# Full-width rectangles in a gated recurrence, and a different order of loads and splits at the ends of a two-layer decoder kernel

## The chip, the core and the metric

The kernel runs on one core of a Trainium2 chip. The core has a matrix engine (TensorE, PE in the profile, with its weight loads shown apart as PEld), a vector engine (DVE), a scalar engine (ACT), a general engine (POOL), and a queue that only issues transfers here (SP). They run side by side and wait for each other through semaphores; each of them takes its own instructions in a fixed order. The metric is the device time of one launch in microseconds.

## The reference

Input x is 1024 tokens of 1024 features; 16 learned meta tokens are put in front. Two layers follow, each `h = h + mixer(rmsnorm(h) * w)`, then a last rmsnorm of the 1024 real tokens. Everything is float32.

Layer 0 (pooling mixer): `v, gate = split(h @ w_in)` with 2048 columns each. In four groups of 512 channels, u is the trailing mean of v over 2, 4, 8 or 16 tokens less v itself. Each group goes through its own 512 x 512 matrix, is scaled, multiplied by `silu(gate)` and goes through `w_out` (2048 to 1024).

Layer 1 (HGRN2): `q, f, i, gate = split(h @ w_in)` with 2048 columns each, in 16 heads of 128. Per head and token the state is `S_t = diag(f_t) S_(t-1) + k_t i_t^T` and the output `o_t = S_t^T q_t`, with `f = lb + (1 - lb) sigmoid(fp)` and `k = (1 - lb) sigmoid(-fp)`. The output is normed per head, multiplied by `silu(gate)` and goes through `w_out`.

## The kernel before

**Precision and products.** The large products run on operands split into a high and a low part (`split`, L147: ACT casts the high part, DVE subtracts it to get the low one), three matmuls for one. The two input products use Strassen's scheme: a pair of weight blocks (`pair`, L213) gives seven operands P1 to P7, made one after the other from two raw tiles of 512 KB, and `products` (L364) runs them in the order P1, P2, P6, P5, P7, P3, P4 against the token operands `T`. The tokens are handled in two halves of 520 (`passes`), each in two chunks of 260 columns; a product is 12 matmuls for one half, 24 for both.

**Weights.** `feed` is a list of functions, each of which makes one split weight operand. `fill` keeps up to three (`LOOK`) made ahead; `need` hands out the next. A split operand lies in one of five "w" buffers (`wslot`), a raw weight tile in one of three "raw" buffers. The first pair of layer 0 stands twice in the list: once for the first half of the tokens, once for the second, since the second half's `T` is not ready when the first half's products start. For layer 1 that holds for the first two pairs.

**Tokens.** `tokens` (L308) gives a list of steps for one half, five tiles of up to 128 tokens. `first(i)` loads the x rows into "ht", in layer 1 adds the transposed output of layer 0 (`ys`, L324, L328) and stores the sum to DRAM (L330), squares it with a running sum on ACT (L331), makes the reciprocal root (DVE L105, POOL L106) and scales the rows (ACT L333). `second(i)`, two steps later, transposes the tile on PE in two halves of a PSUM bank each (L346) and multiplies by the norm weights, half of it on ACT (L349), half on DVE (L351). `make_T` follows: sums and differences of the normed blocks (L277) and their splits.

**The recurrence.** For each head `scan` (L742) lists pieces that are put in between the next head's products; PIECES gives the tick at which each of them is issued, and a tick follows every product (in the last stage every weight tile). Scores inside a chunk of 128 tokens are built in a matrix A: 32 x 32 diagonal blocks by masked 128 x 128 products (L683), then `rect` (L625) at width h = 32 and h = 64, which computes for each chunk the block of h keys by the h queries after them. At h = 32 it does so in two groups of 8 chunk matmuls (keys 0 to 31 and 64 to 95), each with its ACT copy (L636), at h = 64 in one. All groups write the same PSUM bank. These matmuls are plain float32, two instructions each. `states` (L776) makes the chunk sums K^T V: the first from the 16 meta rows (L785), the rest from 128 rows (L787). `outs` multiplies A and V, Q and S (L808, L809), `gated` turns the normed output, multiplies by the gate and stores it to DRAM (L832).

**The last stage.** `out1` (L886) takes the token tiles in three rounds of 3, 3 and 2. For each of 16 heads it reads the gated output back from DRAM (L904), splits it, and multiplies it by `hgrn_w_out`, which is split in the first round and kept. The last head's pieces are issued there, one tick for each weight tile; what has not been issued when the last head's operand is due is issued at once (`flush`, L895).

**Order.** The program's order is a priority. The framework lays out each engine's and each queue's instruction list when the kernel is built, by priority and by when its planner expects operands and buffers; at run time nothing is reordered. Buffers of one tag ("u": 38 of one token-length row each) are handed out in the order in which the program asks for them.

The functions that the change touches:

Of the kernel before, what the change touches and what calls it, by code (L numbers as in the profile page):

```python
# [51 lines left out]
def kernel(  # L52
# [102 lines left out]
    def whole(fast):  # L155
# [24 lines left out]
        def ensure(i):  # L180
            for j in range(len(raws), min(i + 1, len(raw_views))):
                raws[j] = rawtile()
                v = raw_views[j]
                nc.sync.dma_start(raws[j].rearrange("p (a b) -> p a b", b=v.shape[2]), v)

        def fill():
            while feed and len(fed) < LOOK:
                fed.append(feed.pop(0)())

        def need():  # L190
            if not fed:
                fed.append(feed.pop(0)())
            return fed.pop(0)
# [7 lines left out]
        def wslot():  # L201
            return wp.tile([P, 2, 512], F32R, tag="w", name="w", bufs=5)
# [105 lines left out]
        def tokens(p, w, ys=None):  # L308

            hn, held = [], {}  # L310

            def first(i):
                t0, tn = TP[p][i]
                o = t0 - p * PT
                ht, sq = unit("ht"), unit("sq")
                src = meta_tokens if t0 == 0 else x[t0 - META : t0 - META + tn]
                nc.sync.dma_start(ht[:tn, :D], src)
                ssq, r = small("ssq", 3), small("rstd", 3)
# [12 lines left out]
                act.activation(sq[:tn, :D], ht[:tn, :D], AF.Square, accum_out=ssq[:tn, 0:1])  # L331
                rstd_into(r, ssq, tn, 1, D)
                act.activation(sq[:tn, :D], ht[:tn, :D], AF.Copy, scale=r[:tn, 0:1])  # L333
                held[i] = sq

            def second(i):
                if not hn:
                    hn.extend(unit("hn").rearrange("p (k t) -> p k t", k=2) for _ in range(4))
                t0, tn = TP[p][i]
                o = t0 - p * PT  # L340
                xt = held.pop(i)
                for h in range(2):
                    b = atbank().rearrange("p (k t) -> p k t", t=P)
                    for k in range(4):
                        kk = h * 4 + k
                        pe.transpose(out=b[:, k, :tn], in_=xt[:tn, kk * P : (kk + 1) * P], identity=ident[:tn, :tn])  # L346
                    for k in (0, 1):
                        kk = h * 4 + k
                        act.activation(hn[2 * h][:, k, o : o + tn], b[:, k, :tn], AF.Copy, scale=w[:, kk : kk + 1])  # L349
                    ww = w[:, h * 4 + 2 : h * 4 + 4].unsqueeze(2).to_broadcast([P, 2, tn])  # L350
                    vec.tensor_tensor(hn[2 * h + 1][:, :, o : o + tn], b[:, 2:4, :tn], ww, mul)  # L351

            n = len(TP[p])
            steps = []
            for i in range(n + 2):
                def step(i=i):
                    if i < n:
                        first(i)
                    if i >= 2:
                        second(i - 2)  # L360
                steps.append(step)
            return steps + make_T(p, hn)

        def products(passes, m, m2):  # L364
# [3 lines left out]
            for name in PRODUCTS:  # L368
                w = need()
# [180 lines left out]
        def view1(t):  # L550
            return [cols(w_in1, "qfig".index(part) * ME + t // 2) for part in ("qg", "fi")[t % 2]]

        def mixer1(steps):
# [71 lines left out]
            def rect(Q, K0, h):  # L625

                b = atbank()
                for s0 in range(0, P, 2 * h):
                    for c in range(NT):
                        pe.matmul(  # L630
                            b[s0 : s0 + h, c * h : (c + 1) * h],
                            lhsT=K0[:, c * P + s0 : c * P + s0 + h],
                            rhs=Q[:, c * P + s0 + h : c * P + s0 + 2 * h],
                            start=True, stop=True,
                        )
                    act.copy(  # L636
                        A.rearrange("p (c t) -> p c t", t=P)[s0 : s0 + h, :, s0 + h : s0 + 2 * h],
                        b[s0 : s0 + h, : NT * h].rearrange("p (c i) -> p c i", i=h),
                    )
# [102 lines left out]
            def scan(n, Q, K, F, ti):  # L742
# [6 lines left out]
                def turn_v():  # L749
                    V = tl["V"] = unit("V")[:, :SEQ].rearrange("p (c v) -> p c v", v=P)  # L750
                    Vm = tl["Vm"] = cst.tile([P, P], F32, tag="Vm", name="Vm", bufs=2)
                    for b0 in (0, 4, 8):
# [42 lines left out]
                def outs():  # L795
# [5 lines left out]
                    ssq, r = small("ssq", 3), small("rstd", 3)  # L801
# [21 lines left out]
                def gated():  # L823
# [8 lines left out]
                    nc.sync.dma_start(a_dram[n], og)  # L832
# [53 lines left out]
        def out1():  # L886
# [6 lines left out]
            def prep(r, n):  # L893
# [9 lines left out]
                ar = half("ar").rearrange("p a b -> p (a b)")[:, : nt * P]  # L903
                nc.sync.dma_start(ar, a_dram[n][:, t0 * P : (t0 + nt) * P])  # L904
# [21 lines left out]
            for r, (tt0, nt) in enumerate(ROUNDS):  # L926
                ps = {}
                for n in range(HEADS - 3):
# [7 lines left out]
                    tick()  # L936
                fetch((r + 1) * HEADS + 2)
                late = [ready.pop((r, n)) for n in range(HEADS - 3, HEADS)]
                for i in range(nt):
# [5 lines left out]
                    ssq, rs = small("ssq", 3), small("rstd", 3)  # L945
# [27 lines left out]
        early(1, ME, lambda t: (cols(w_in0, t), cols(w_in0, ME + t)))  # L973
# [10 lines left out]
        spread(tokens(1, nw[0]))  # L984
        c0 = v_gate(0)
        products((0,), *c0)
        flush()
        products((1,), *c0)
# [5 lines left out]
        a = grp_stage(0)  # L994
        hs = out_stage(0, a)
# [4 lines left out]
        mixer1(tokens(1, nw[1], hs))  # L1000
# [38 lines left out]
```

## Time and profile before

| what | value |
|---|---|
| median of 3 runs | 1800.05 us (1799.66 to 1802.28) |
| the profiled execution | 1796.19 us, span 1794.4 us |
| PE busy | 1701.6 us, 95% of the span |
| DVE, ACT, POOL busy | 1238.1, 807.7, 51.8 us |
| granted TensorE clock, mean | 0.981 |

The span is what the profiler sees of one execution; the device time has 1.8 us more around it. In views by instruction a row gives start, length, engine, line, operation, operands, count, and in brackets how long the engine had been idle and what ended that. In the chain of waits a row gives start, length and what the end of the program waited for at that time. The granted clock is 1.00 at full speed and 0.50 at half.

### The profile page before, as it was taken

The page shows a single profiled execution, that of the slowest core. Times are in us where ns is not written, and L with a number is a line of the kernel's source. Part 1 is how long each engine was busy: PE and PEld are TensorE (multiplying, and loading weights), DVE is VectorE, ACT ScalarE, POOL GpSimd, SP SyncE. Part 2 cuts the span into 40 slices and gives each one's busy share as a digit, 9 for nine tenths or more (in the row PEclk, how much of TensorE's full clock was granted, in tenths as well). Part 3 has the DMA queues.
Part 4 walks back from the last instruction along what each step waited for, and adds up shares of the span by engine and source line. Part 5 has one row for each costly group of instructions (what it writes and reads, how often), then busy time and mean ns, then how long its engine had stood idle before and what let it go on. Part 6 is the DMA issues. An engine that isn't in the chain of part 4 may idle for free.

```text
span 1794.4 us, 32938 instructions
## 1 busy us (share of the span) xinstructions
PE 1701.6 (95%) x13571; PEld 1634.3 (91%) x13571; DVE 1238.1 (69%) x1948; ACT 807.7 (45%) x1783; POOL 51.8 (3%) x70
## 2 busy tenths in 40 slices
PE   3699999999999999699999999999999999999897
PEld 2599999999999899599999999999999999987686
DVE  4676777789226824798887887887887887783332
ACT  5643333335225624545544555544554544553221
POOL 0110000000000000000000000000000000000000
PEclk9699999999999999899999999999999999999999
DMA  3232333349337434122212212222212212351531
GB/s 91 71 113 96 107 107 110 104 148 302 107 119 232 123 95 125 63 86 78 66 61 83 84 48 78 66 70 73 83 50 81 72 60 72 108 191 50 166 106 40
DMA packets 194083, 178.68 MB, mean 100 GB/s; under 512 B 7189, under 2 KB 167013, under 8 KB 193925
## 3 DMA queue, kind: packets, MB, share of 16 engines
q1 hardware_dynamic: 193925, 176.49, 31.0%
q8 instruction: 109, 1.79, 0.4%
q14 instruction: 49, 0.40, 0.1%
HBM read 134.13 MB, written 42.34 MB: 98 GB/s over the span
## 4 chain that ended last, share of the span: by engine, by line
PE 86%; DVE 6%; DMA 3%; ACT 3%; issue 1%; POOL 1%; SPq 0%; DVEq 0%; POOLq 0%; ACTq 0%
PE mm L383 17%; PE mm L385 17%; PE mm L384 17%; PE mm L505 5%; PE mm L506 5%; PE mm L507 5%; PE mm L922 3%; PE mm L924 3%; PE mm L923 3%; PE at L630 2%; DMA ht<-in_x_dram 2%; PE at L683 2%; PE at L787 2%; PE at L809 2%; PE at L808 2%
## 5 line engine op out<-in xcount | busy, mean ns | idle before, releaser
L383 PE MATMUL mm<-Th,w 128*128 128x260 f32 x2688 | 781.1, 291 | 24.9 <-ACT Th L148 9.4
L385 PE MATMUL mm<-Th,w 128*128 128x260 f32 x2688 | 768.9, 286 | 0.6 <-DVE w L149 0.5
L384 PE MATMUL mm<-Tl,w 128*128 128x260 f32 x2688 | 765.2, 285 | 1.9 <-DVE Tl L149 1.9
L383 PEld LDWEIGHTS mm<-Th,w 128*128 128x128 f32 x2688 | 512.6, 191 | 31.6 <-ACT Th L148 10.8
L384 PEld LDWEIGHTS mm<-Tl,w 128*128 128x128 f32 x2688 | 513.2, 191 | 3.0 <-DVE Tl L149 2.9
L385 PEld LDWEIGHTS mm<-Th,w 128*128 128x128 f32 x2688 | 512.4, 191 | 2.3 <-DVE w L149 1.4
L149 DVE TENSOR_TENSOR w<-raw,w 128x512 fp32r<-128x512 f32 x351 | 235.2, 686 | 182.7 <-ACT w L148 180.5
L148 ACT CAST w<-raw 128x512 fp32r<-128x512 f32 x351 | 212.8, 620 | 166.2 <-PE mm L507 106.4
L505 PE MATMUL mm<-a,w 128*128 128x260 f32 x512 | 145.0, 283 | 0.0
L506 PE MATMUL mm<-a,w 128*128 128x260 f32 x512 | 144.6, 282 | 0.0
L507 PE MATMUL mm<-a,w 128*128 128x260 f32 x512 | 144.2, 282 | 0.0
L389 ACT COPY P<-mm 128x520 f32<-128x520 f32 (+1 forms) x153 | 85.9, 562 | 120.1 <-PE mm L385 118.6
L148 ACT CAST w<-S 128x512 fp32r<-128x512 f32 x102 | 61.3, 620 | 119.4 <-PE mm L385 61.2
L664 DVE RECIPROCAL F<-X 128x260 f32<-128x260 f32 x64 | 111.3, 1758 | 0.0
L922 PE MATMUL mm<-woh,w 128*128 128x512 f32 x256 | 103.7, 405 | 5.3 <-ACT w L148 3.6
L924 PE MATMUL mm<-woh,w 128*128 128x512 f32 x256 | 102.2, 400 | 0.0
L923 PE MATMUL mm<-wol,w 128*128 128x512 f32 x256 | 102.0, 398 | 0.0
L506 PEld LDWEIGHTS mm<-a,w 128*128 128x128 f32 x512 | 96.5, 188 | 0.0
L507 PEld LDWEIGHTS mm<-a,w 128*128 128x128 f32 x512 | 96.4, 188 | 0.0
L505 PEld LDWEIGHTS mm<-a,w 128*128 128x128 f32 x512 | 96.4, 188 | 0.0
L106 POOL TENSOR_TENSOR rstd<-rstd,nhalf 128x1 f32<-128x1 f32 (+4 forms) x44 | 44.2, 1005 | 1723.5 <-DVE rstd L105 1712.1
L505 PE MATMUL mm<-u,w 128*128 128x260 f32 x256 | 73.9, 289 | 0.5 <-ACT u L148 0.5
(147 smaller groups left out, 2509.1 us busy)
## 6 DMA issues: line engine op xcount, KB each, us to landing
raw<-in_hgrn_w_in_dram SPq DMA_DIRECT2D x68, 512.0 KB, 4.3
raw<-in_pool_w_in_dram SPq DMA_DIRECT2D x34, 512.0 KB, 4.3
raw<-in_pool_w_out_dram SPq DMA_DIRECT2D x32, 512.0 KB, 4.1
u_dram<-d SPq DMA_DIRECT2D x16, 520.0 KB, 2.7
ur<-u_dram SPq DMA_DIRECT2D x32, 260.0 KB, 5.0
sgh<-s_dram SPq DMA_DIRECT2D x32, 260.0 KB, 4.8
raw<-in_pool_w_grp_dram SPq DMA_DIRECT2D x16, 512.0 KB, 3.7
gl<-g_dram SPq DMA_DIRECT2D x32, 256.0 KB, 5.6
```

Source lines behind the costliest of these rows:

```text
L148: act.copy(hi, src)
L149: vec.tensor_tensor(lo, src, hi.bitcast(F32), sub)
L383: pe.matmul(o, lhsT=w[:, 0, ks], rhs=th[:, k], start=first, stop=False, **kw)
L384: pe.matmul(o, lhsT=w[:, 0, ks], rhs=tl[:, k], start=False, stop=False, **kw)
L385: pe.matmul(o, lhsT=w[:, 1, ks], rhs=th[:, k], start=False, stop=k == 3, **kw)
L505: pe.matmul(o, lhsT=w[:, 0, ks], rhs=xs[k][:, 0, cs], start=first and k == 0, stop=False)
L506: pe.matmul(o, lhsT=w[:, 0, ks], rhs=xs[k][:, 1, cs], start=False, stop=False)
L507: pe.matmul(o, lhsT=w[:, 1, ks], rhs=xs[k][:, 0, cs], start=False, stop=last and k == 3)
L664: vec.reciprocal(iX[:, s], X[:, s])
L922: pe.matmul(ps[i][nh], lhsT=w[:, 0, ts], rhs=wh[:, s], start=n == 0, stop=False)
L923: pe.matmul(ps[i][nh], lhsT=w[:, 0, ts], rhs=wl[:, s], start=False, stop=False)
L924: pe.matmul(ps[i][nh], lhsT=w[:, 1, ts], rhs=wh[:, s], start=False, stop=n == HEADS - 1)
```

## The change

1. `rect` multiplies, for each of the 8 chunks, all 128 key rows by 64 queries: at h = 32 the two odd blocks of 32, at h = 64 the upper 64. The result has 128 rows, of which the needed blocks are copied as before.
2. The 16-row state product gets 128 rows: POOL sets the two operands to zero before ACT writes the 16 rows.
3. In the start, the x rows of the first half are loaded first. The first two raw weight tiles wait for the reciprocal root of the second token tile, through a small DVE copy into them; behind them come the x rows of the second half.
4. The first pair of layer 0 stands once in the list. Its seven operands are kept from the first half's products for the second half's. Two of them lie in "u" buffers, and a count (`limit`) holds back further splits until kept buffers come free.
5. In layer 0 the scaling of the token rows goes from ACT to DVE. In both layers a token tile is transposed into one PSUM buffer of two banks; in layer 0 one of four pairs is multiplied on ACT and three on DVE, in layer 1 two and two.
6. In layer 1, the first three x tiles of the second half are loaded in the out stage of layer 0, and `second(i)` comes three steps after `first(i)`.
7. In the last stage there are two ticks for each weight tile. The last head's gated output stays in SBUF: it is neither stored nor read back.

The diff, cut to its core:

```diff
         def ensure(i):
             for j in range(len(raws), min(i + 1, len(raw_views))):
                 raws[j] = rawtile()
+                if j < 2:
+                    vec.tensor_copy(raws[j][:8, 0:1], stat[0][:8, 0:1])
...
+        limit, spare = [7], [2]
         def fill():
-            while feed and len(fed) < LOOK:
+            while feed and len(fed) < LOOK and limit[0] > 0:
                 fed.append(feed.pop(0)())
+                limit[0] -= 1
...
         def wslot():
+            if spare[0] > 0:
+                spare[0] -= 1
+                return unit("w", F32R)[:, :1024].rearrange("p (h k) -> p h k", h=2)
...
+        def load_tokens(p, i):
+            t0, tn = TP[p][i]
+            ht = unit("ht")
+            nc.sync.dma_start(ht[:tn, :D], meta_tokens if t0 == 0 else x[t0 - META : t0 - META + tn])
+            return ht
...
-                act.activation(sq[:tn, :D], ht[:tn, :D], AF.Copy, scale=r[:tn, 0:1])
+                if i == 1:
+                    stat[0] = r
+                if ys is None:
+                    vec.tensor_scalar(sq[:tn, :D], ht[:tn, :D], r[:tn, 0:1], None, mul)
+                else:
+                    act.activation(sq[:tn, :D], ht[:tn, :D], AF.Copy, scale=r[:tn, 0:1])
...
+                b = mmbanks().rearrange("p h (k t) -> p (h k) t", t=P)
+                for k in range(KD):
+                    pe.transpose(out=b[:, k, :tn], in_=xt[:tn, k * P : (k + 1) * P], identity=ident[:tn, :tn])
+                for j in range(4):
+                    ks = slice(2 * j, 2 * j + 2)
+                    if j == 0 or (j == 2 and ys is not None):
+                        for k in (2 * j, 2 * j + 1):
+                            act.activation(hn[j][:, k % 2, o : o + tn], b[:, k, :tn], AF.Copy, scale=w[:, k : k + 1])
+                    else:
+                        ww = w[:, ks].unsqueeze(2).to_broadcast([P, 2, tn])
+                        vec.tensor_tensor(hn[j][:, :, o : o + tn], b[:, ks, :tn], ww, mul)
...
-            for name in PRODUCTS:
-                w = need()
+            for i, name in enumerate(PRODUCTS):
+                if kept is not None and len(kept) == 7:
+                    w = kept[i]
+                    if i >= 2:
+                        limit[0] += 1
+                else:
+                    w = need()
+                    if kept is not None:
+                        kept.append(w)
...
+                if m == 5 and p == 1:
+                    ahead.extend(load_tokens(1, i) for i in range(3))
...
             def rect(Q, K0, h):
-                b = atbank()
-                for s0 in range(0, P, 2 * h):
-                    for c in range(NT):
-                        pe.matmul(
-                            b[s0 : s0 + h, c * h : (c + 1) * h],
-                            lhsT=K0[:, c * P + s0 : c * P + s0 + h],
-                            rhs=Q[:, c * P + s0 + h : c * P + s0 + 2 * h],
-                            start=True, stop=True,
-                        )
-                    act.copy(...)
+                b = atbank().rearrange("p (c i) -> p c i", i=64)
+                q4 = Q.rearrange("p (c b i) -> p c b i", c=NT, i=h)
+                for c in range(NT):
+                    pe.matmul(b[:, c], lhsT=K0[:, c * P : (c + 1) * P], rhs=q4[:, c, 1::2], start=True, stop=True)
+                A3 = A.rearrange("p (c t) -> p c t", t=P)
+                for i, s0 in enumerate(range(0, P, 2 * h)):
+                    act.copy(A3[s0 : s0 + h, :, s0 + h : s0 + 2 * h], b[s0 : s0 + h, :, i * h : (i + 1) * h])
...
+                            pool.memset(Vm, 0.0)
...
+                            pool.memset(KT[:, 7], 0.0)
...
-                                pe.matmul(b[:, c], lhsT=KT[:META, 7], rhs=Vm[:META], start=True, stop=True)
+                                pe.matmul(b[:, c], lhsT=KT[:, 7], rhs=Vm, start=True, stop=True)
...
-                    nc.sync.dma_start(a_dram[n], og)
+                    if n < HEADS - 1:
+                        nc.sync.dma_start(a_dram[n], og)
+                    else:
+                        last.append(og)
...
                         proj(ps, w, n, i)
-                    tick()
+                        if i < 2:
+                            tick()
...
-        early(1, ME, lambda t: (cols(w_in0, t), cols(w_in0, ME + t)))
+        early(0, ME, lambda t: (cols(w_in0, t), cols(w_in0, ME + t)))
...
-        for fn in tokens(0, nw[0]):
+        hts = [[load_tokens(0, i) for i in range(len(TP[0]))]]
+        for i, fn in enumerate(tokens(0, nw[0], hts=hts[0])):
             fn()
-        fill()
+            if i == 1:
+                ensure(1)
+                hts.append([load_tokens(1, i) for i in range(len(TP[1]))])
+            if i == len(TP[0]):
+                fill()
...
-        mixer1(tokens(1, nw[1], hs))
+        mixer1(tokens(1, nw[1], hs, ahead, 3))
```

## Rows read from the trace of the kernel before

**Rows 1.** The page: busy times, and the costliest groups (busy, mean ns).

```profile
PE 1701.6 (95%) x13571; PEld 1634.3 (91%) x13571; DVE 1238.1 (69%) x1948; ACT 807.7 (45%) x1783; POOL 51.8 (3%) x70
L149 DVE TENSOR_TENSOR w<-raw,w 128x512 fp32r<-128x512 f32 x351 | 235.2, 686 | 182.7 <-ACT w L148 180.5
```

**Rows 2.** Windows: stretch, length, busy PE, PEld, DVE, ACT, POOL, clock, DMA, GB/s.

```profile
14.00:38.00 24.00, 10.65 (x49) 8.88 (x50) 9.85 (x24) 17.50 (x39) 2.58 (x4) 1.00 0.27 84
38.00:99.00 61.00, 39.13 (x203) 34.13 (x203) 41.96 (x73) 38.04 (x73) 9.85 (x9) 0.72 0.24 74
710.00:740.00 30.00, 20.44 (x125) 17.18 (x124) 16.89 (x35) 18.28 (x43) 2.10 (x3) 0.77 0.40 139
740.00:770.00 30.00, 20.86 (x139) 18.68 (x138) 28.61 (x48) 16.34 (x33) 0.00 (x0) 0.93 0.16 44
```

**Rows 3.** Chain of waits in one head: start, length, what.

```profile
1080.98 1.07 PE at L630 x16
...
1129.80 0.12 PE mm L385
1129.92 0.62 PE at L630 x16
1130.54 0.33 PE mm L383
...
1134.44 1.07 PE at L630 x16
...
1142.31 0.41 PE at L785 x2
1142.73 1.76 PE at L787 x14
...
1150.26 0.22 PE at L808 x2
```

**Rows 4.** Groups by form, weight loads: count, busy us, mean ns, idle before.

```profile
L808 PEld LDWEIGHTS at<-V,A 128*128 128x128 f32 x256 | 39.0, 192 | 0.2
L630 PEld LDWEIGHTS at<-Q,K 128*32 128x32 f32 x512 | 18.6, 113 | 4.9 <-issue 0.4 <-ACT A L636 0.4
L757 PEld LDWEIGHTS at<-ident,ti 128*128 128x128 f32 x128 | 14.7, 142 | 0.1
L757 PEld LDWEIGHTS at<-ident,ti 128*16 128x16 f32 x16 | 1.4, 87 | 2.7 <-ACT V L759 2.7
```

**Rows 5.** Timeline, weight loads of a 16-token tile's transposes in layer 1.

```profile
569.54 0.32 PEld L346 LDWEIGHTS at<-ident,sq 16*128 16x128 f32 x4 [0.32 <-DVE ht L328]
```

**Rows 6.** Timeline of the start, ACT and DVE.

```profile
11.63 1.14 ACT L148 CAST w<-raw 128x512 fp32r<-128x512 f32 x2 [1.58 <-DMA raw<-in_pool_w_in_dram]
...
14.89 1.06 ACT L331 ACTIVATE sq<-ht 128x1024 f32<-128x1024 f32 x1 [1.08 <-DMA ht<-in_x_dram]
...
37.36 0.40 DVE L351 TENSOR_TENSOR hn<-at,vecs 128x240 f32<-128x240 f32 x1
```

**Rows 7.** Lines by source, whole span: count, ns min/median/max, first and last start, forms.

```profile
L333 ACT ACTIVATE sq<-ht,rstd x20: 1144/1150/1158, 12.7 to 732.4; 128x1024 f32<-128x1024 f32 x14, 16x1024 f32<-16x1024 f32 x2, 120x1024 f32<-120x1024 f32 x2, 8x1024 f32<-8x1024 f32 x2
L349 ACT ACTIVATE hn<-at,vecs x80: 246/360/407, 19.9 to 739.2; 128x128 f32<-128x128 f32 x56, 128x16 f32<-128x16 f32 x8, 128x120 f32<-128x120 f32 x8, 128x8 f32<-128x8 f32 x8
L588 DVE TENSOR_SCALAR F<-F,oml,lb x34: 408/550/555, 741.0 to 1574.0; 128x520 f32<-128x520 f32 x30, 128x260 f32<-128x260 f32 x4
```

**Rows 8.** Timeline, entry of layer 1, SP and DVE.

```profile
722.31 0.42 SPq L317 DMA_DIRECT2D ht<-in_x_dram  x1
...
728.17 1.28 DVE L328 TENSOR_TENSOR ht<-ht,at 128x512 f32<-128x512 f32 x2 [1.96 <-DMA ht<-in_x_dram]
```

**Rows 9.** Timeline, end of the first round of the last stage, PE.

```profile
1656.38 0.62 PE L829 MATMUL at<-ident,on 128*128 128x128 f32 x2 [1.80 <-ACT on L821]
...
1665.30 0.50 PE L922 MATMUL mm<-woh,w 128*128 128x512 f32 x1 [3.65 <-ACT w L148]
```

**Rows 10.** Windows, the same end.

```profile
1666.00:1670.00 4.00, 4.00 (x12) 3.23 (x12) 2.19 (x5) 1.54 (x3) 0.00 (x0) 0.59 0.96 305
```

More of the change, by code (lines that the diff above doesn't have):

```diff
@@ L192, in need @@
                 fed.append(feed.pop(0)())
+                limit[0] -= 1
             return fed.pop(0)
@@ L306, in make_T, with tokens @@
             return [s1, s2, s3, s4, s5, s6]
-        def tokens(p, w, ys=None):
+        stat = [None]
+        def load_tokens(p, i):
[3 more added lines that the diff above has]
+            return ht
+        def tokens(p, w, ys=None, hts=None, lag=2):
             hn, held = [], {}
@@ L314, in first @@
                 o = t0 - p * PT
[L315 to L318, printed above, removed]
+                ht, sq = hts.pop(0) if hts else load_tokens(p, i), unit("sq")
+                ssq, r = small("ssq", 3), small("rstd", 4)
                 if ys is not None:
@@ L341, in second @@
                 xt = held.pop(i)
[L342 to L351, printed above, removed]
+                b = mmbanks().rearrange("p h (k t) -> p (h k) t", t=P)
[9 more added lines that the diff above has]
+                        vec.tensor_tensor(hn[j][:, :, o : o + tn], b[:, ks, :tn], ww, mul)
             n = len(TP[p])
             steps = []
-            for i in range(n + 2):
+            for i in range(n + lag):
                 def step(i=i):
@@ L358, in step, with products @@
                         first(i)
-                    if i >= 2:
-                        second(i - 2)
+                    if i >= lag:
+                        second(i - lag)
                 steps.append(step)
             return steps + make_T(p, hn)
-        def products(passes, m, m2):
+        def products(passes, m, m2, kept=None):
             s = slice(passes[0], passes[-1] + 1)
             a = x_ = None
-            for name in PRODUCTS:
-                w = need()
+            for i, name in enumerate(PRODUCTS):
[7 more added lines that the diff above has]
+                        kept.append(w)
                 if name == "P1":
@@ L551, in view1 @@
             return [cols(w_in1, "qfig".index(part) * ME + t // 2) for part in ("qg", "fi")[t % 2]]
+        last = []
         def mixer1(steps):
@@ L800, in outs @@
                     on = tl["on"] = [half("on").rearrange("p a b -> p (a b)")[:, :512].rearrange("p (c v) -> p c v", v=P) for _ in range(2)]
-                    ssq, r = small("ssq", 3), small("rstd", 3)
+                    ssq, r = small("ssq", 3), small("rstd", 4)
                     tl["r"] = r
@@ L902, in prep @@
                 t0, nt = ROUNDS[r]
-                ar = half("ar").rearrange("p a b -> p (a b)")[:, : nt * P]
-                nc.sync.dma_start(ar, a_dram[n][:, t0 * P : (t0 + nt) * P])
+                ts = slice(t0 * P, (t0 + nt) * P)
+                if n < HEADS - 1:
+                    ar = half("ar").rearrange("p a b -> p (a b)")[:, : nt * P]
+                    nc.sync.dma_start(ar, a_dram[n][:, ts])
+                else:
+                    ar = last[0][:, ts]
                 w = wslot()
@@ L944, in out1 @@
                         proj(ps, w, HEADS - 3 + j, i)
-                    ssq, rs = small("ssq", 3), small("rstd", 3)
+                    ssq, rs = small("ssq", 3), small("rstd", 4)
                     for nh in range(2):
@@ L977, in whole @@
         early(2, 2 * HEADS, view1)
-        for fn in tokens(0, nw[0]):
-            fn()
-        fill()
+        hts = [[load_tokens(0, i) for i in range(len(TP[0]))]]
+        for i, fn in enumerate(tokens(0, nw[0], hts=hts[0])):
+            fn()
+            if i == 1:
[3 more added lines that the diff above has]
+                fill()
         if fast:
             later(40, make_mask)
-        spread(tokens(1, nw[0]))
-        c0 = v_gate(0)
-        products((0,), *c0)
+        spread(tokens(1, nw[0], hts=hts[1]))
+        c0, kept = v_gate(0), []
+        products((0,), *c0, kept)
         flush()
-        products((1,), *c0)
+        products((1,), *c0, kept)
+        limit[0] = len(feed)
         for t in range(1, ME):
@@ L994, in whole @@
         a = grp_stage(0)
+        ahead = []
         hs = out_stage(0, a)
```

4 lines of the change are left out of this document (removed).

## The prediction, made before the change was run

> **What bounds the kernel now.** I read the page's busy line first, then windows over the stretches in which TensorE is idle, then the chain of waits inside one recurrence head, then the timeline at the start, at the entry of the second layer and at the end. TensorE is busy for 1701.6 of 1794.4 us [rows 1], so 92.8 us are idle, and the rest can shrink only by giving TensorE less to do. The idle time is not spread: 13.4 us lie in 14 to 38, 21.9 in 38 to 99, 18.7 in 710 to 770 [rows 2]; the last head's return costs 1.80 and 3.65 more [rows 9]. Inside a head there is none: the groups and products follow each other on TensorE without a gap, and a head is 1134.44 - 1080.98 = 53.46 us [rows 3]. So three edits aim at idle time, and one (rectangles and the 16-row state product) at TensorE's own work.
>
> **The steady heads.** A product step costs 0.12 us; a group costs its own row plus what the product behind it takes above 0.12 [rows 3]. The 32-wide level runs as two groups of 16 instructions (each matmul is two), each 0.62 + (0.33 - 0.12) = 0.83, so 1.66. The 64-wide level is 1.07 + 0.2 = 1.27. Together 2.93 us a head. New: each level is 8 matmuls, 16 instructions, with 128 stationary columns and 64 moving ones. No row has that form. From below: the 64-wide group's own pace, 1.07 / 16 = 0.067 each, if the moving side sets it. From above: load and stream one after the other. What does a load cost? By form it takes 113 ns for 32 columns and 192 for 128 [rows 4], 0.82 ns a column, so 105 ns for 128 columns beyond a fixed part. That this slope is a pace and not a latency is shown by the transposes: their loads go from 87 to 142 ns between 16 and 128 columns, 0.49 ns a column, 63 ns for 128, and where the moving side is only 16 columns four of them take 0.32 us, (0.32 - 0.14) / 3 = 0.06 each [rows 5]. So a narrow moving side leaves the load as the bound. The existing full-size form, 128 columns against 128, takes 0.22 for two instructions (one of sixteen such rows of the output step [rows 3]); I take its 0.111 each for the new form too. A level is then 16 x 0.111 = 1.78, both 3.55, without the 0.2 us that stands behind the narrow groups (none stands behind the full-size ones). That is 3.55 - 2.93 = +0.62 us a head: this edit loses. Bounds: 32 x 0.067 = 2.14, -0.79 a head; one after the other 32 x (0.105 + 0.067) = 5.5, +2.6 a head.
>
> The Trainium skill, "TensorE: Matmul & The Clock Gate", section "LDWEIGHTS (loading the stationary operand)", says that a load's time goes with its columns, P / 1.2 ns, and speaks against this edit: estimated from it, 32 x 0.107 = 3.4 us a head, +0.5, about what the rows give. [...]
>
> The state product: the 16-row pair and the 14 full ones take 0.41 + 1.76 = 2.17 [rows 3]; 16 full ones at 0.111 are 1.78. That saves 0.39 a head (nothing if the extra is not due to the 16 rows, 0.41 at most). Its two memsets run on POOL, which is busy for 51.8 us in all [rows 1]; they stand before small ACT copies, but their tile is free long before, so I cost them at nothing; were POOL late, ACT's queue would wait a few tenths per head, and ACT is busy for only 45% [rows 1]. Heads: 16 x (0.62 - 0.39) = **+4 us** (from -19 to +36).
>
> **The start.** Today the first x tile is squared at 14.89, 3.3 us after the first weights were cast at 11.63 [rows 6], since two weight loads are queued ahead of it. With x first it takes the weights' place: about 11.6. The weights are then issued when the second tile's rstd is there, near 14, and come while the other tiles are worked on; their splits are not needed before the first operand is split. From 14.89 to the last normed tile at 37.36 [rows 6] the four big tiles take 22.5 us, mostly ACT, which is busy 17.5 of the 24 us from 14 to 38: square 1.06, scale 1.15, four copies of 0.36 a tile [rows 2, 6, 7]. The scale goes to DVE: TENSOR_SCALAR takes 0.41 at 260 and 0.55 at 520 columns [rows 7], so 0.55 + 504 x 0.00053 = 0.82 at 1024 (1.15, ACT's, as upper bound). One pair of ACT copies per tile becomes one DVE product of 0.40 [rows 6]. A tile is then 1.06 + 2 x 0.36 = 1.8 on ACT and 0.82 + 3 x 0.40 = 2.0 on DVE. Four tiles: 11.6, plus 6 for the first one's way through (today 22.5 less three quarters of it, 5.6), plus 3 x 2.0, is 24; with DVE also splitting weights I take 27. Gain to there 10.4 (bounds 5 and 13).
>
> From 38 to 99 (both single passes of the first pair, between them the second half's tokens) DVE is busy 41.96 of 61 us, ACT 38.04 [rows 2]. Gone: 7 splits of 0.69 [rows 1] and 4 sums of that length on DVE, 7.5 us, their ACT casts and two loads. Added on DVE: 5 x 0.82 scales and 5 products of 0.40, 6; and some 3.5 of splits that now fall behind the last tile. So DVE has 44 us, ACT only 38 - 4 - 6 - 3 = 25. DVE becomes the bound of this stretch. At the 95% it reaches in 740 to 770 [rows 2] it needs 46 us, at today's 69% 64; I take 80%, since the x rows of the second half are now there early and no cast waits for a weight slot in between: 55. Against 61 that gains 6 (bounds 15 and -3). The start: **-16 us** (-2 to -28). What is late next is DVE: the differences and splits of T.
>
> **Entry of the second layer.** Each x tile is issued behind the store of the tile before; the last one at 722.31 lands for DVE at 728.17 [rows 8], and four such round trips follow each other, while DVE is busy only 16.9 of 30 us in 710 to 740 [rows 2]. Three tiles now come ahead, during the out stage, so two round trips remain (the fourth and fifth tile are still loaded in their step, behind SP's stores): the chain shortens by 2 x 7 us less the time in which the other tiles compute, some 10. But from 740 on DVE runs at 95% and takes up the work that was waiting, so I count **-8 us** (0 to -12). The three tiles fit the ring of 38 buffers by my count; if not, they delay the next out tile.
>
> **The end.** The last head's chain is flushed at the end of the first round: TensorE waits 1.80 for ACT, later 3.65 for the first split of the tile that goes to DRAM and back, and then runs at a granted clock of 0.59 from 1666 to 1670 [rows 9, 10], 4 x 0.41 = 1.6 us lost. With two ticks per weight tile all 18 pieces are through after nine of 13 tiles, and the tile stays in SBUF. All three go: **-7 us** (-3 to -9; more pieces per us press on DVE, where splits run three tiles ahead). The other parts (transposes in one double bank, more small buffers, split counts) change which bank is taken and I cost them at 0, +-2.
>
> **Sum.** -16 - 8 - 7 + 4 = -27 on the profiled execution, 1796.2 (span 1794.4): 1769. The median shown, 1800.05, is 3.9 above that execution; runs after should scatter likewise, and I put the time at 1771.
>
> **Rivals.** (a) The moving side, not the load, sets the new rectangles' pace: 0.067 instead of 0.111, 32 x 0.044 x 16 = 23 us less, 1748. For it: no row has this form. Against: rows 5. [...] Chance 0.14. (b) The idle time turns into other waits: DVE keeps 69% in the start (gain 8 in all), the layer entry gains 3, the end 4, the heads cost 4: 1796 - 11 + 2 = 1787. For it: ACT and DVE today wait for each other in order in that stretch. Chance 0.18. (c) Slower: the wide load is not overlapped with so short a stream, 0.172 an instruction: +2.6 - 0.39 = 2.2 a head, 36 us in place of 4, against gains of 31: +5, 1803. It decides from about 0.163 an instruction on. Against: the narrow forms pay the larger of the two and not the sum (0.067 at 64 against a load slope of 0.053). Chance 0.05. (d) An edit misses its aim, the kept weights above all: their two extra buffers could stall the ring, and with (b) it ends within 0.2%, 3.6 us, which is what a measurement here can tell: chance 0.03.
>
> **How the numbers follow.** Forecast 0.60, with 1760 to 1783 as its own range. The range of 1751 to 1789 leaves out most of (a), all of (c) and (d): 0.2. Faster: 0.60 + 0.14 + 0.17 = 0.91; same 0.03; slower 0.06.
>
> **What would show it.** In a head: a rectangle row of about 1.78 for 16 instructions and a pitch of 53.7 (52.3 under (a), 55.7 under (c)). First square near 11.6, last normed tile near 27, no idle TensorE behind 83 instead of 99, DVE over 75% before that. No wait of about 2 us for the last x tile, and steady work from about 762 instead of 770. No clock below 1 at the end of the first round. I am wrong if the pitch falls, if the start still ends at 95 or later, or if the rings stall in the out stage.

## The result, and the profile after

The changed kernel takes 1767.17 us (median of 4 runs, 1765.72 to 1768.34) against 1799.86 for the kernel before on the same chip (4 runs, 1795.89 to 1802.28): a ratio of 0.982, 95% interval 0.9801 to 0.9839. The forecast was 1771. The profiled execution took 1768.34 us, its span 1766.6. One of four executions of a later kernel, e7 below, took 3375.68 us; e7's row is that of the other three.

The page's busy line answers to [rows 1]: TensorE's idle time fell from 92.8 to 70.5 us, while its work fell only by 5.5.

```profile
PE 1696.1 (96%) x13315; PEld 1647.8 (93%) x13315; DVE 1239.5 (70%) x1959; ACT 786.3 (45%) x1746; POOL 55.2 (3%) x102
```

The windows of [rows 2] and [rows 10] after the change (stretch, length, busy PE, PEld, DVE, ACT, POOL, clock, DMA share, GB/s). In 38 to 99 TensorE is busy 50.55 instead of 39.13, and DVE 51.57 instead of 41.96 of 61 us; in 740 to 770 TensorE has 1.3 us idle instead of 9.1; the clock from 1666 to 1670 is full. The changed kernel is ahead, by 17 us at the end of layer 0's out stage and 28 at its own end, so from 710 on the same times hold other work. The last head's last transposes, at 1656 to 1659 before, stand at 1613 to 1616 now; the row from 1600 to 1620 holds them, at a full clock.

```profile
14.00:38.00 24.00, 10.62 (x46) 9.24 (x45) 14.65 (x34) 10.58 (x25) 2.03 (x3) 1.00 0.52 159
38.00:99.00 61.00, 50.55 (x342) 47.19 (x341) 51.57 (x92) 32.03 (x63) 6.41 (x9) 0.83 0.17 53
710.00:740.00 30.00, 21.60 (x138) 20.19 (x139) 26.64 (x44) 19.11 (x39) 0.00 (x0) 0.83 0.12 36
740.00:770.00 30.00, 28.72 (x232) 27.74 (x230) 26.71 (x41) 14.92 (x33) 0.00 (x0) 1.00 0.28 80
1600.00:1620.00 20.00, 20.00 (x105) 16.23 (x104) 9.32 (x17) 11.32 (x33) 1.64 (x1) 1.00 0.51 177
1666.00:1670.00 4.00, 4.00 (x19) 3.22 (x18) 0.56 (x1) 0.51 (x1) 0.00 (x0) 1.00 0.11 33
```

The chain of waits in one head, which answers to [rows 3]: a rectangle level is one row of 1.73, and the product behind it takes 0.18, 0.06 more than the usual 0.12, so 1.73 + 0.06 = 1.79 a level; the state product is 0.22 + 1.56 = 1.78.

```profile
1110.26 1.73 PE at L664 x16
1111.99 0.18 PE mm L413
...
1114.93 1.73 PE at L664 x16
1116.66 0.18 PE mm L413
...
1123.36 0.22 PE at L815 x2
1123.58 1.56 PE at L817 x14
```

DVE's and then ACT's timeline at the start, which answer to [rows 6] (start, length, line, what, in brackets the idle time before it and what ended it). Both engines stand for 7 us and more until the first weights land at 21.36, although the third x tile needs neither of them; its square, on ACT, is queued behind the cast of the weight sum and begins at 23.34. The last normed tile, L374, starts its last three products at 33.62.

```profile
12.82 0.75 DVE L353 TENSOR_SCALAR sq<-ht,rstd 128x1024 f32<-128x1024 f32 x1 [0.67 <-POOL rstd L106]
13.49 0.19 DVE L185 COPY raw<-rstd 8x1 f32<-8x1 f32 x2
21.36 0.69 DVE L244 TENSOR_TENSOR S<-raw 128x512 f32<-128x512 f32 x1 [7.67 <-DMA raw<-in_pool_w_in_dram]
...
25.34 0.75 DVE L353 TENSOR_SCALAR sq<-ht,rstd 128x1024 f32<-128x1024 f32 x1 [0.67 <-POOL rstd L106]
...
33.62 1.03 DVE L374 TENSOR_TENSOR hn<-mm,vecs 128x240 f32<-128x240 f32 x3
```

```profile
22.82 0.62 ACT L148 CAST w<-S 128x512 fp32r<-128x512 f32 x1 [10.85 <-DVE S L245]
23.34 1.05 ACT L348 ACTIVATE sq<-ht 128x1024 f32<-128x1024 f32 x1
```

At the entry of layer 1 the last x tile's row of [rows 8] stands at 705.20 now, without a wait. In the list of TensorE's waits from 1560 to the end one entry is left, 0.8 us for ACT; neither of the two of [rows 9] is there.

Where the time went, by landmarks of the two traces. They differ by 27.8 us, the medians by 32.7: the trace before lies 3.7 below its median, the one after 1.2 above, and no landmark can place those 4.9. The first read of u, behind the whole first stage, moved from 393.0 to 375.5 (-17.5); up to the last product of the out stage (697.2 before, 680.2 now) 0.5 was given back; from there to the first head's state product 4.3 were gained, 124.6 becoming 120.3; the heads' pitch rose from 53.49 to 53.82, +0.33 a head; from the 11th head to the end 437.65 became 427.81, of which four longer heads hide 1.3, so the end gained 11.2.

### The profile page after: what moved, and what is told of

The parts are those of the page before. It is cut to its first block, busy times and chain, and to the rows that moved or that the text cites. A ratio compares the mean times of both kernels' runs of the same rounds, so it can differ in the third digit from the quotient of the medians.

```text
span 1766.6 us, 32378 instructions
## 1 busy us (share of the span) xinstructions
PE 1696.1 (96%) x13315; PEld 1647.8 (93%) x13315; DVE 1239.5 (70%) x1959; ACT 786.3 (45%) x1746; POOL 55.2 (3%) x102
## 4 chain that ended last, share of the span: by engine, by line
PE 88%; DVE 6%; ACT 2%; DMA 2%; issue 1%; SPq 0%; POOL 0%; DVEq 0%; POOLq 0%; ACTq 0%
PE mm L413 17%; PE mm L415 17%; PE mm L414 17%; PE mm L535 5%; PE mm L536 5%; PE mm L537 5%; PE mm L959 3%; PE mm L960 3%; PE mm L961 3%; PE at L664 3%; PE at L711 2%; PE at L838 2%; PE at L839 2%; PE at L817 1%; DMA ht<-in_x_dram 1%
## 5 line engine op out<-in xcount | busy, mean ns | idle before, releaser
L959 PE MATMUL mm<-woh,w 128*128 128x512 f32 x256 | 101.4, 396 | 0.0
L961 PE MATMUL mm<-woh,w 128*128 128x512 f32 x256 | 100.4, 392 | 0.0
```

The lines of the kernel that those rows point to most:

```text
L959: pe.matmul(ps[i][nh], lhsT=w[:, 0, ts], rhs=wh[:, s], start=n == 0, stop=False)
L961: pe.matmul(ps[i][nh], lhsT=w[:, 1, ts], rhs=wh[:, s], start=False, stop=n == HEADS - 1)
```

## The experiments

Each kernel is the changed one with one edit. The columns: median time; ratio to the kernel before, timed on the same chip; when the first u is read (the start); and the pitch, from the second to the eleventh head's state product, divided by nine.

| run | us | ratio, 95% interval | first u | pitch |
|---|---|---|---|---|
| before | 1799.86 | | 393.0 | 53.49 |
| after | 1767.17 | 0.982 (0.9801-0.9839) | 375.5 | 53.82 |
| e1 old rectangles | 1758.72 | 0.977 (0.9754-0.9787) | 376.8 | 53.18 |
| e2 half the moving side | 1771.22 (one run) | | 378.0 | 53.82 |
| e3 16-row state product | 1774.70 | 0.9865 (0.9848-0.9881) | 379.1 | 54.19 |
| e4 weights behind all x | 1764.06 | 0.9806 (0.979-0.9822) | 373.9 | 53.71 |
| e5 first pair twice | 1773.03 | 0.9854 (0.9834-0.9874) | 381.3 | 53.74 |
| e6 scale on ACT | 1769.84 | 0.9834 (0.9818-0.9851) | 378.5 | 53.78 |
| e7 last head through DRAM | 1769.58 | 0.9829 (0.9809-0.9849) | 378.3 | 53.82 |
| e8 one tick | 1773.68 | 0.986 (0.9834-0.9885) | 375.8 | 53.82 |
| e9 no x ahead | 1776.05 | 0.9865 (0.9847-0.9884) | 377.7 | 53.81 |
| e10 early load, late use | 1760.81 | 0.9781 (0.9763-0.98) | 369.5 | 53.73 |
| e12 weights first | 1768.09 | 0.982 (0.9801-0.984) | 375.8 | 53.82 |
| e11 = e1 + e10 | 1751.32 | 0.9725 (0.9708-0.9742) | 370.0 | 53.07 |

Two warnings on how to read it. The starts of after, e1, e2, e3, e7, e8 and e9 are the same code, and their first u lies between 375.5 and 379.1. So up to 3.6 us of any total may be the start's own scatter, though a late start can be made up again before the heads (e3, e9), and small effects are read from the stage that the edit touches. And a trace is one execution: those of the experiments lie between 1.2 us below their medians and 2.0 above, so that stages and totals need not add up closer than that.

**e1, the old rectangles.**

```
-  for c in range(NT):
-      pe.matmul(b[:, c], lhsT=K0[:, c * P : (c + 1) * P], rhs=q4[:, c, 1::2], ...)
+  for s0 in range(0, P, 2 * h):
+      for c in range(NT):
+          pe.matmul(b[s0 : s0 + h, c * h : (c + 1) * h], lhsT=K0[:, c * P + s0 : c * P + s0 + h],
+                    rhs=Q[:, c * P + s0 + h : c * P + s0 + 2 * h], ...)
 ...
```

> Only the rectangles go back to their old form (per level the narrow groups of key rows against their own queries, at h=32 two groups of 16 instructions, at h=64 one); everything else stays as changed. My theory (128 stationary columns a load set the new form's pace, so the edit loses): a head gets 3.58 - 2.93 = 0.65 us shorter, pitch 53.81 -> 53.16, 16 heads 10 us, time 1757 (1755 to 1760). The rows come back as 0.62 twice with 0.2 behind each, and 1.07 with 0.2. Rival (the edit pays because the moving side is cheap, or because fewer groups stop the chain): no gain or a loss, 1767 to 1775.

The pitch fell by 0.64. The chain of waits shows the old rows and the 0.2 behind each:

```profile
1108.22 0.62 PE at L664 x16
1108.85 0.32 PE mm L413
...
1110.01 0.62 PE at L664 x16
1110.63 0.32 PE mm L415
...
1112.75 1.08 PE at L664 x16
1113.83 0.32 PE mm L413
```

16 x 0.64 = 10.3 us, and the time fell by 8.5, with a start 1.3 later. The rectangles are a loss inside a change that gains.

**e2, half the moving side.**

```
-  pe.matmul(b[:, c], lhsT=K0[:, c * P : (c + 1) * P], rhs=q4[:, c, 1::2], ...)
+  pe.matmul(b[:, c, :h] if h == 32 else b[:, c], lhsT=K0[:, c * P : (c + 1) * P],
+            rhs=q4[:, c, 1:2:2] if h == 32 else q4[:, c, 1::2], ...)
 ...
-      act.copy(A3[...], b[s0 : s0 + h, :, i * h : (i + 1) * h])
+      act.copy(A3[...], b[s0 : s0 + h, :, 0:h])
```

> At the 32-wide level only the first odd block of 32 queries of each head part moves, 32 moving columns an instruction instead of 64, against the same 128 stationary columns; this leaves out half of that level's queries, and the second ACT copy takes the first block's columns. The 64-wide level is unchanged and is the measure beside it. My theory (the load sets the pace): the 32-wide level's row stays at 1.7 to 1.75 us for 16 instructions, pitch 53.8, time within 1 us of 1767. Rival (the moving columns set it, or load and stream add up): the row falls by a quarter to a half, to 0.9 to 1.3, pitch 52.9 to 53.4, time 1753 to 1760.

In the chain of waits, the first row is the level with 32 moving columns, the second that with 64:

```profile
1113.05 1.71 PE at L665 x16
1114.75 0.20 PE mm L413
...
1117.71 1.73 PE at L665 x16
1119.45 0.17 PE mm L413
```

Half the moving columns change nothing: 0.107 against 0.108 an instruction, and the pitch stays. So the 128 stationary columns set the pace here. The total, 3 us above the level expected, is the start's scatter (first u at 378.0, the first head 2.8 later than after's).

**e3, the 16-row state product.**

```
-  pool.memset(Vm, 0.0)
 ...
-  pool.memset(KT[:, 7], 0.0)
 ...
-  pe.matmul(b[:, c], lhsT=KT[:, 7], rhs=Vm, start=True, stop=True)
+  pe.matmul(b[:, c], lhsT=KT[:META, 7], rhs=Vm[:META], start=True, stop=True)
```

> Only the state product of the 16-row tile goes back to 16 rows (and the two memsets go). My theory (a group that changes the row count pays about 0.2 us on either side): the product returns from 1.78 to 2.17 a head, +0.39 x 16 = 6.2 us, time 1773.4 (1771 to 1775). Rival (that extra was not due to the 16 rows but to what precedes the group): no change, 1766 to 1768.

The chain of waits has the old rows again, the pair and the 14 behind it both longer:

```profile
1124.81 0.41 PE at L813 x2
1125.22 1.76 PE at L815 x14
```

The pitch rose by 0.37, 16 heads 5.9 us. The time rose by 7.5, the trace by 5.3. The first u came 3.6 later, but that is not in the total: the first head's state product begins at 800.1, against 800.5 in after, and from there to the end the trace is 5.7 longer.

**e4, weights behind all x rows, and e10, early load, late use.** e4 moves the gate of the two loads and their place in program order behind the fifth x tile; e10 moves the place alone. In both, the reading in of the second half's x rows, which stands behind the two loads, moves with them:

```
 def first(i):                          # e4 only
-    if i == 1: stat[0] = r
+    if i == 4: stat[0] = r
 ...
 for i, fn in enumerate(tokens(...)):   # e4 and e10
-    if i == 1: ensure(1) ...
+    if i == 4: ensure(1) ...
```

> The first two weight loads of the first layer wait for the rstd of the fifth (last) x tile instead of the second, so their sums and casts stand behind all five tiles' squares and scalings in the queues of DVE and ACT. My theory of why the last normed tile came at 34.6 instead of 27 (the weight sums stand in DVE's queue ahead of the third tile and wait 7.7 us for the landing at 21.4): with them behind, the last normed tile comes at about 26 to 28, the third square at about 16 instead of 23.3, and TensorE is steady some 5 us earlier: 1762 (1758 to 1765). Rival (DVE's work, not its order, bounds the stretch, or the weights now simply land later): the idle comes back behind the last tile, time 1765 to 1771.

> The first two weight loads still wait for the second x tile's rstd, but are asked for in program order behind the fifth tile, so that their sums and casts stand behind all tiles in the queues of DVE and ACT, and the loads start as early as in the changed kernel. My theory (the harm was the order of the queues and not the work): the last normed tile at about 22.6 as with the later loads, the weight sums start at about 22 with no wait for a landing above 1 us, against 26.7 there, and the time is 1761 (1758 to 1764). Rival (the lead of the first half is swallowed by DVE and ACT in the second half's tokens, whatever its size): 1763 to 1767.

DVE's timeline in e4: the last normed tile's products end at 22.6, even before my 26 to 28, and then DVE waits for the weights.

```profile
20.43 2.17 DVE L374 TENSOR_TENSOR hn<-mm,vecs 128x256 f32<-128x256 f32 x6
26.69 0.69 DVE L244 TENSOR_TENSOR S<-raw 128x512 f32<-128x512 f32 x1 [4.08 <-DMA raw<-in_pool_w_in_dram]
```

In e10 the weights land at 22.37, when DVE has little else to do, and the last normed tile ends at 24.6:

```profile
22.37 0.69 DVE L244 TENSOR_TENSOR S<-raw 128x512 f32<-128x512 f32 x1 [0.53 <-DMA raw<-in_pool_w_in_dram]
...
23.89 0.71 DVE L374 TENSOR_TENSOR hn<-mm,vecs 128x240 f32<-128x240 f32 x2
```

e4 gained 3.1 (1.6 at the first u; its interval overlaps that of after), e10 6.4 (6.0 at the first u, clear of the scatter). The order of the queues was the harm, as the theory had it. That e10's last tile comes 10 us earlier and its first u only 6 fits DVE's share, below: from 60 to 83 DVE is busy 21.99 of 23 us in e10. In e4, e5 and e10 the pitch is also 0.1 lower, some 1.5 us in all, and no run explains that.

**e12, weights first.**

```
+  ensure(1)            # and no gating copy in ensure
   hts = [[load_tokens(0, i) for i in range(len(TP[0]))]]
   ...
-      ensure(1)
```

> The first two weight loads are issued ahead of all x rows, without a gate, as before the change; all else as changed (first pair split once, scaling on DVE). My theory (what counted at the start was that DVE's weight sums stood in its queue before they had landed, not which load was first): the sums run at about 12 without a long wait, the first big x tile is squared at about 15 instead of 11 to 12, the last normed tile comes at about 28 instead of 34.6, with all first splits already done: 1763 (1760 to 1766), so the part of the change that put x first lost, as it stands. Rival (x first is worth its 4 us, in the first square and in all after it): 1770 to 1773.

Neither came: 1768.09, the same as x first. ACT's timeline shows why. Its first instructions are now the weight casts, and they wait for a landing and DVE's sums until 15.16; the first, small x tile, which the changed kernel squares at about 9, is squared at 16.73:

```profile
15.16 1.14 ACT L148 CAST w<-S 128x512 fp32r<-128x512 f32 x2 [10.39 <-DVE S L245]
16.21 0.61 ACT L148 CAST w<-raw 128x512 fp32r<-128x512 f32 x1
16.73 1.05 ACT L348 ACTIVATE sq<-ht 16x1024 f32<-16x1024 f32 x1
```

My theory was right on the queue and wrong on the size: with the weights first the queue is blocked at its head instead of its middle. The last normed tile ends at 32.0 (34.6 after), and the first u is read at 375.8, within the scatter. So putting x first bought nothing that can be told, as long as the sums stand in the way.

**e5, the first pair split twice, and e6, the scaling on ACT.**

```
-  limit, spare = [7], [2]                           # e5
+  limit, spare = [10000], [0]
-  early(0, ME, lambda t: ...
+  early(1, ME, lambda t: ...
-  c0, kept = v_gate(0), []
+  c0, kept = v_gate(0), None

-  if ys is None: vec.tensor_scalar(sq, ht, r, mul)  # e6
-  else: act.activation(sq, ht, AF.Copy, scale=r)
+  act.activation(sq, ht, AF.Copy, scale=r)
```

> The first pair's weights are fed and split a second time for the second pass, as before the change (no kept operands, no limit on early splits, no spare buffers); x rows still come first. My theory (DVE bounds the stretch up to the steady point, so 7 splits and 4 sums of 0.68 us on DVE count in full): +7.5, time 1775 (1771 to 1779), DVE above 90% busy from 38 to the steady point, which comes some 7 us later. Rival (the second splits fit into DVE's waits for ACT): within 2 us of 1767.

> The scaling by rstd in the first layer goes back from DVE (0.74 us a tile) to ACT (1.15). My theory (DVE is at 87 to 92% from 38 to 83, ACT below 70%): the four large tiles of the second half free 3 us of DVE there, but square and scale of one tile then follow each other on ACT, +0.4 us a tile and the in-order copies behind: about even, 1767 (1763 to 1771). Rival (the scaling on ACT was what made the start slow before the change): +5 to +8, 1772 to 1775.

The window 60 to 83 (columns as above) of after, e5 and e6, in this order:

```profile
60.00:83.00 23.00, 17.59 (x105) 16.16 (x105) 21.04 (x36) 10.65 (x21) 3.67 (x4) 0.78 0.03 12
```

```profile
60.00:83.00 23.00, 14.22 (x80) 12.29 (x78) 22.08 (x38) 13.90 (x28) 6.31 (x4) 0.85 0.03 12
```

```profile
60.00:83.00 23.00, 15.40 (x101) 13.50 (x99) 19.38 (x34) 14.62 (x28) 4.22 (x5) 0.93 0.03 12
```

With the second splits DVE is busy 96% of it, and TensorE 3.4 us less; the first u comes at 381.3, 2.2 behind the latest of the unchanged starts and 5.8 behind the earliest. The time rose by 5.9 (the trace by 3.5), as I expected (7.5, 4 to 12). The scaling on ACT frees DVE and gives the time to ACT: first u at 378.5, inside the scatter, time +2.7. About even, as expected; moving it to DVE did not make the start fast.

**e9, no x ahead.**

```
-  if m == 5 and p == 1:
-      ahead.extend(load_tokens(1, i) for i in range(3))
...
-  mixer1(tokens(1, nw[1], hs, ahead, 3))
+  mixer1(tokens(1, nw[1], hs))
```

> At the entry of the second layer no x tile is loaded ahead and the lag of the token steps is 2 again. My theory (the entry gained 3.9 us between the two traces, all from the missing round trips): +4, time 1771 (1769 to 1774), and the wait for the last x tile of about 2 us is back near 710 to 730. Rival (DVE at over 90% bounds the entry, and the early x bought nothing there; the 3.9 came from elsewhere): 1766 to 1768.

Windows over the entry, first of after, then of e9:

```profile
640.00:720.00 80.00, 73.03 (x582) 71.47 (x581) 38.98 (x73) 39.13 (x81) 3.30 (x5) 0.96 0.40 122
720.00:740.00 20.00, 12.30 (x75) 10.89 (x75) 19.13 (x31) 11.27 (x21) 0.00 (x0) 0.83 0.00 1
```

```profile
640.00:720.00 80.00, 65.26 (x510) 62.98 (x509) 34.26 (x63) 34.93 (x70) 3.12 (x5) 0.87 0.35 109
720.00:740.00 20.00, 14.82 (x107) 13.86 (x106) 18.21 (x29) 12.50 (x24) 0.00 (x0) 0.91 0.19 54
```

Without the early x TensorE loses 7.8 us before 720 (e9's waits there are 10.4 for ACT's scaling and 4.2 for the x tile), and gets 2.5 back in 720 to 740, where in the changed kernel DVE, busy 19.13 of 20, has become the bound. The last product of the out stage ends at 680.1 in e9 and at 680.2 in after, so the 2.2 by which e9's first u came later had been made up by then. From there to the first head's state product e9 takes 127.4 us and after 120.3: 7.1 more, well above the theory's +4. The total rose by 8.9, the trace by 7.5; the rest of the latter lies behind the 11th head.

**e7, the last head through DRAM, and e8, one tick.**

```
-  if n < HEADS - 1:            # e7, at the store and at the load
+  if True:

-  if i < 2: tick()             # e8, one tick per weight tile
+  tick()
```

> The last head's output is stored to DRAM and read back by the final product, as before the change; two ticks per weight tile stay. My theory (with two ticks the last head is through four tiles before the round's end, so the trip is hidden): no change, 1766.5 to 1769, no wait of TensorE for the first split of that tile. Rival (the trip stood on the path whenever it began): a wait of about 3.6 us and a lower clock behind it, 1771 to 1773.

> One tick instead of two per weight tile in the final product's first round; the last head's output stays in SBUF. My theory (the pace of the last head's pieces, flushed at the end of the round, caused the larger part of the 11 us that the end gained): the stretch from the last head to the end grows by 3 to 6 us, with an idle TensorE before the last transposes at about 1650: 1771 (1769 to 1774). Rival (the trip to DRAM and back was the whole of it): within 1 us of 1767.

From the 11th head to the end e7 takes 427.85 against 427.81: the trip to DRAM costs nothing when two ticks run. Its total is 2.4 higher, with a first u 2.8 later. e8 takes 433.45, 5.6 more, and TensorE's waits from 1560 on (line, releaser, us, times, longest) are these; after has only the first of them, with 0.8:

```profile
PE at L785 <- ACT V L787: 2.4, 1, 2.4
PE at L859 <- ACT on L851: 1.8, 1, 1.8
PE mm L959 <- DVE hres L985: 1.7, 2, 1.4
```

**e11, old rectangles with early load and late use.** The edits of e1 and e10 together.

> The old rectangles (as in e1) and the early load with late use (as in e10) together; all else as changed. My theory (one acts in the heads, the other before the steady point, so they add): pitch 53.16, first u read at about 369.5 to 371, 1767.2 - 9 - 6.4 = 1752 (1749 to 1754). Rival (the gains overlap, or the start's scatter eats one): 1755 to 1759.

They add: 8.5 + 6.4 = 14.9 by the two runs, 15.9 measured. This version beats both kernels.

## Why the prediction was right, point by point

**The heads** were right to a tenth: +0.23 a head forecast, +0.33 measured; the levels 3.58 instead of 3.55, the state product 1.78 as forecast. The price came from two rows: the 0.111 of the full-size form, and the pace of loads in front of short transposes [rows 3, 5]. e2 confirms the reason, and refutes rival (a) together with (c): neither the moving columns nor a sum of load and stream sets the pace. The Trainium skill, "TensorE: Matmul & The Clock Gate", section "LDWEIGHTS (loading the stationary operand)", gives P / 1.2 ns for P columns, by estimate 107 ns for 128, and the 0.107 to 0.108 an instruction of e2 agrees. Its section "Back-to-back issue gap" gives a formula by the moving columns, but calls that the isolated gap, too small at few columns for want of the load; e2, where the load and not the moving columns sets the pace, bears that caveat out.

**The start** came out at -17.5 (-14 to -17.5 by the scatter) for -16, from two terms that were both mis-sized, in opposite directions. The last normed tile was to come at 27, 10.4 earlier; it came 3 earlier. The step of the prediction that failed was "the weights are then issued when the second tile's rstd is there ... and come while the other tiles are worked on": the loads did, but the sums and casts that use them stood in the in-order queues ahead of those tiles. e4 and e10 show it: the same work in another order ends that tile at 22.6 and 24.6. The second term was to gain 6, and gained 14.4. My DVE work was right: from 34.6 to 83 it is busy 43.6 us, 44 forecast. It ran at 90% of that stretch where I took 80%. Rival (b), idle time turned into other waits, is the true story of the first term and false for the second. So the sum was right partly by luck. Behind the last tile the forecast's sign came: from 78 to 99 TensorE is busy throughout, where "no idle TensorE behind 83" was forecast.

What the start owes to which edit is only partly settled. The pair split once is worth about 2 to 6 us (e5); x first and the scaling on DVE nothing that the scatter lets one see (e12, e6). e5, with the pair split twice, still reads its first u 11.7 us ahead of the kernel before (393.0 to 381.3). These 11.7 fall to edits that no run undid (the second half's x rows read in early, the double bank for transposes with its new shares of ACT and DVE), or to a combination; this stays open. The traces hold a lead. Behind 38 us, TensorE's waits at the transposes of the second half's tokens (line, releaser, us, times, longest) were these before the change:

```profile
PE at L346 <- ACT sq L333: 3.8, 1, 3.8
PE at L346 <- DVE hn L351: 2.4, 2, 1.6
```

After it there is one:

```profile
PE mm L366 <- DVE hn L374: 0.8, 1, 0.8
```

In the same stretch DVE waited 5.0 us for ACT's half of the norm products before and does not wait for it any more, in after or in e5. That points to the transposes, but is not shown by a run.

**The entry of layer 1** gained 4.3 from the last product of the out stage on, 3.8 from the first u on, for -8 (inside 0 to -12). The mechanism was right, and e9 prices it: without the x tiles ahead the entry takes 7.1 longer. TensorE's idle time falls by 7.8 there (I had some 10), and 2.5 go back where DVE is the bound (I allowed 2). The term missed is another: e9 needs 127.4 us for the entry, where the kernel before needed 124.6, so something else in the change costs some 2.7 there (one trace each; the traces with x ahead scatter by 1.4). No run shows what; the transposes, with their new shares of ACT and DVE, are a candidate.

**The end** gained 11.2 for -7 (bound -9). The three terms seen all went. I had missed that the faster ticks also remove stalls ahead of them: 2.3 for ACT's V, now 0.8, the low clock around it (0.97 over 1545 to 1600 before, 1.00 after), and 1.7 for the residual. e7 and e8 split it: the ticks are worth 5.6 with the tile in SBUF. The store and load that [rows 9] shows waiting 3.65 cost nothing once the ticks come early, so keeping the last head in SBUF was needed only with one tick. That the trip with one tick costs the other 5.6 was not run by itself.

**The sum.** By the traces -17.5 (start), -3.8 (entry), -11.2 (end) and +4.6 (heads) make up the 27.8, for -16, -8, -7 and +4. The entry fell short by as much as the end came out over, so the agreement of the total with -27 is luck there too; right were the signs, the heads' price and most of the waits that would go. The 2 us added for the scatter of runs did not come: the trace after lies above its median, not below.

**Rival (d)**, an end within 3.6 us of the kernel before, is refuted. But an edit that misses its aim there was, one that I had not named: x first.

## What to carry to other kernels

Price a matmul by its load as well as by its stream. Here an instruction with 128 stationary columns took 0.107 to 0.111 us whether 32, 64 or 128 columns moved, so widening the stationary side to save instructions lost where the moving side was short. A load that is moved later needs its consumers moved too, since on an in-order engine the first instruction that waits for it holds up everything behind it. And where two edits remove the same wait, undo each alone before crediting both.

## What was not expected of the hardware

The same start varied by 3.6 us at the first u, and the granted clock went with it. Here are the windows 50 to 60 of after and of e3:

```profile
50.00:60.00 10.00, 9.53 (x72) 8.59 (x70) 7.16 (x23) 6.66 (x18) 2.74 (x5) 0.89 0.13 33
```

```profile
50.00:60.00 10.00, 9.53 (x46) 8.68 (x44) 6.00 (x16) 6.02 (x14) 2.19 (x4) 0.50 0.27 74
```

TensorE is busy 9.53 us in both, but at 0.50, the lower level of 1.2 GHz throughout, it gets through 46 matmuls instead of 72. In the 10 us ahead it had been busy 5.8 and 4.4 us. Of seven profiles, the three at 0.82 to 0.89 read their first u at 375.5 to 376.8, the four at 0.50 to 0.62 at 377.7 to 379.1.

What comes first is open. The landing of the first weights does not sort the runs: DVE began the first weight sum at 21.36 in after and 22.46 in e3, but at 22.62 in e1, which kept 0.82, and at 21.53 in e9, which had 0.62. Nor does TensorE's busy time from 40 to 50, 5.5 us in e1 and 5.9 in e9. And the lag need not last: in e3, 3.6 behind at the first u, the last product of the out stage ends at 680.5, against 680.2 in after.
